# Cross-entropy of 256 x 32000 logits: the first 64 rows in three loads instead of two

## The chip, the cores and the metric

The kernel runs on one core of one Trainium2 chip. The metric is the time of one execution on the device in microseconds. The kernel before takes 82.59 us, the median of four runs (82.54 to 82.75).

A core has several engines that run side by side, each with its own instruction queue: TensorE (PE in the profile), VectorE (DVE), ScalarE (ACT), GpSimd (POOL) and SyncE (SP). Here SP only issues transfers. Sixteen DMA engines move data between the chip's main memory (HBM) and the core's own memory (SBUF), which has 128 partitions.

## What is computed

For each of 256 rows, the logarithm of the sum of the exponentials of the row, less the logit of the row's label:

```python
def reference(logits, labels):           # [256, 32000] float32, [256] int32
    log_probs = logits - np.max(logits, axis=-1, keepdims=True)
    log_probs = log_probs - np.log(np.sum(np.exp(log_probs), axis=-1, keepdims=True))
    return np.array([-log_probs[i, labels[i]] for i in range(batch)])
```

The kernel leaves out the maximum: it computes log(sum(exp(x)) * exp(-x[label])), which is the same number. The input is 32.77 MB, each element is read once, and the output is 1 KB.

## The kernel before

**Groups and chunks.** The rows are cut into four groups of 64, 128, 32 and 32 rows (`GROUPS`, L18). A group of k rows lies over all 128 partitions: each row is cut into 128/k stretches, one to a partition. The first group so has 16000 columns on each partition, the second 32000, the last two 8000 each. `LOADS` (L20 to L25) cuts the columns of each group into chunks, and each chunk is one load from HBM: 14 in all, numbered through. A load of n columns is 128 rows of 4n bytes.

**Buffers.** Chunks 0 to 5 have a buffer each (`SLOTS`, L30). Chunks 6 and 7 use the buffers of chunks 2 and 3 again. The six chunks of the last group (`TAIL`, from chunk 8) lie side by side in the buffer of chunk 1 (`TAIL_SLOT`, L32).

**Work on a chunk** (`step`, L270). ScalarE takes the exponential in place (`exps`, L208 to L215). For the first group the same instruction also sums over the columns into one column of `parts`. For chunks 2 to 11 (`HALVED`, L41) VectorE adds the two halves of the chunk and sums the result into `near` (L294). Chunks 12 and 13 are summed by ScalarE again. For every chunk after the first group, TensorE multiplies the sums of the partitions by `weights` (L300), which gives one number for each row. For the first group that is done once, after its last chunk: a sum over `parts` (L284) and one product (L285). Its logarithm (L222) is taken after the exponential of the next chunk.

**The label's logit.** ACT's queue loads the labels (L229). POOL computes the addresses and gathers the logits of the labels from HBM (L250). In the step of chunk `GATHERED` (1) ScalarE takes exp(-x) of these (L274), and VectorE and TensorE build `weights` from them (L276 to L282). That is why the row's sum comes out multiplied by exp(-x[label]).

**Warm-up.** In the step of chunk `WARM_FROM` (7) TensorE gets sixteen products whose result nobody uses (L291).

**Order.** All is in an order written out by hand. SP first issues the loads of chunks 0 to 5. Then comes a loop (L307) that, for each later load, first writes out the steps up to the one that frees its buffer. So load 6 waits for VectorE's half-sum of chunk 2, load 7 for that of chunk 3, and the tail loads stand behind load 7 on SP's queue; their buffer is free as soon as ScalarE has worked on chunk 1. Each load also has a completion counter. There are eight of these, handed round among the loads, the transfer of the labels and the store of the result. A load that takes a used counter waits for the transfer that had it before.

**Start and end.** `begin_first_load_before_barrier` puts the first load ahead of the barrier at the start. `end_before_store_lands` (L60) puts SP's waits for everything else ahead of the store of the result, so that the barrier and the clearing of the counters run while the store is under way. The last instruction is SP's wait for the store. Because the clearing must leave out the store's counter, and this is the last one of the range here, the range is shortened by one (L91, L92).

Of the kernel before, what the change touches and what calls it, by code (L numbers as in the profile page):

```python
# [17 lines left out]
GROUPS = [64, 128, 32, 32]  # L18

LOADS = [  # L20
    [1024, 14976],
    [8896, 8192, 8320, 6592],
    [4736, 3264],
    [2496, 1824, 1344, 992, 736, 608],
# [2 lines left out]
GROUP_OF = [g for g, ns in enumerate(LOADS) for _ in ns]  # L27


SLOTS = [0, 1, 2, 3, 4, 5, 2, 3]  # L30
TAIL = len(SLOTS)
TAIL_SLOT = 1  # L32
SKIP = 32


WARM_FROM = 7
WARM = 16

GATHERED = 1

HALVED = range(2, 12)  # L41


def begin_first_load_before_barrier(nc):
# [15 lines left out]
def end_before_store_lands(nc):  # L60

    body, end = nc.m.functions[0].blocks[1:3]
    insts = list(body.instructions)
    at = max(k for k, i in enumerate(insts) if i.opcode == "DMACopy")
    store = insts[at]
    (landed,) = store.sync_info.on_update
    assert store.engine == mybir.EngineType.SP  # L70
    assert all(i.engine != mybir.EngineType.SP or i.opcode != "DMACopy" for i in insts[at + 1:])

    rest = list(end.instructions)
    drain = rest.pop(0)
    assert drain.engine == mybir.EngineType.SP and drain.opcode == "Drain"
    waits = list(drain.sync_info.on_wait)
    (full,) = [w for w in waits if w.id == landed.id]

    held = {w.id: w.wait_value for w in store.sync_info.on_wait}
    waits = [w for w in waits if w.id != landed.id and held.get(w.id) != w.wait_value]  # L80
    assert not list(drain.sync_info.on_update)
    insts.insert(at, mybir.InstEventSemaphore(
        name=drain.name, engine=drain.engine, debug=drain.debug, ins=[], outs=[],
        sync_info=mybir.SyncInfo(on_wait=waits, on_update=[]),
    ))

    clear = next(k for k, i in enumerate(rest) if i.opcode == "ISA")
    old = rest[clear]
    assert old.op_name == "EVENT_SEMAPHORE_RANGE_CLEAR"
    words, fields = list(old.instr), dict(old.ant_dict)  # L90
    assert words[14] == fields["range_last"] == landed.id  # L91
    words[14] = fields["range_last"] = landed.id - 1  # L92
    rest[clear] = mybir.InstISA(
        isa_opcode=old.isa_opcode, instr=tuple(words), verify=old.verify, op_name=old.op_name,
        ant_dict=fields, ant_isa_is_sequencer_only=old.ant_isa_is_sequencer_only,
        name=old.name, engine=old.engine, debug=old.debug, ins=[], outs=[],
    )

    assert all(i.opcode in ("Drain", "EventSemaphore") for i in rest[clear + 1:])
    del rest[clear + 1:]  # L100
    rest.append(mybir.InstEventSemaphore(
        name=nc.get_next_instruction_name(), engine=mybir.EngineType.SP, debug=old.debug,
        ins=[], outs=[],
        sync_info=mybir.SyncInfo(
            on_wait=[full],
            on_update=[mybir.SyncUpdate(
                sync_type="semaphore", id=full.id, ant_name=full.ant_name,
                update_mode="sem-sub-imm", update_value=full.wait_value,
            )],
        ),  # L110
    ))
    body.instructions = insts
    end.instructions = rest
# [3 lines left out]
def kernel(  # L117
# [6 lines left out]
    nc = tc.nc  # L124
    nc.at_finalize(begin_first_load_before_barrier)
    nc.at_finalize(end_before_store_lands)
    B, C = logits.shape
    assert B == P * ROWS == sum(GROUPS)
# [19 lines left out]
    width = {}  # L148
    for i, s in enumerate(SLOTS):
        width[s] = max(width.get(s, 0), CHUNKS[i])  # L150
    width[TAIL_SLOT] = max(width[TAIL_SLOT], sum(CHUNKS[TAIL:]))


    place = []
    for i, s in enumerate(SLOTS):
        skip = SKIP if s == 0 else 0
        t = big.tile([P, skip + width[s]], F32, name=f"x{i}", tag=f"slot{s}")
        place.append(t[:, skip:skip + CHUNKS[i]])
    assert all(width[s] % 64 == 0 for s in width)
    tail = big.tile([P, width[TAIL_SLOT]], F32, name="x_tail", tag=f"slot{TAIL_SLOT}")  # L160
    for i in range(TAIL, last + 1):
# [3 lines left out]

    assert HALVED[0] == last_of[0] + 1 and HALVED[-1] == last - 2
    assert all(CHUNKS[i] % 2 == 0 for i in HALVED)
    parts = small.tile([P, len(LOADS[0])], F32, name="parts")
    row_0 = small.tile([P, 1], F32, name="row_0")
    near = {i: small.tile([P, 1], F32, name=f"near{i}") for i in range(HALVED[0], last + 1)}  # L170
    res = small.tile([1, B], F32, name="res")
# [36 lines left out]
    def exps(i):  # L208
        if i in HALVED:
            acc = None  # L210
        elif i > last_of[0]:
            acc = near[i][:, :]
        else:
            acc = parts[:, i:i + 1]
        nc.scalar.activation(out=place[i], in_=place[i], func=AF.Exp, accum_out=acc)  # L215
# [5 lines left out]
    def logs(rows, sums):  # L221
        nc.scalar.activation(out=res[0:1, rows], in_=sums, func=AF.Ln)  # L222

    with tc.manual_schedule():
        first = len(set(SLOTS))
        for i in range(first):
# [43 lines left out]
        def step(i):  # L270
            exps(i)
            g = GROUP_OF[i]
            if i == GATHERED:
                nc.scalar.activation(out=eg[:, :], in_=g_at[:, :], func=AF.Exp, scale=-1.0)  # L274
                for r in range(ROWS):
                    nc.vector.tensor_scalar_mul(diag[r][:, :], ident[:, :], eg[:, r:r + 1])  # L276

                for r in range(ROWS):
                    nc.tensor.matmul(  # L279
                        spread[:, r * P:(r + 1) * P], ones[:, :], diag[r][:, :], start=True, stop=True  # L280
                    )
                nc.vector.tensor_mul(out=weights[:, :], in0=holds[:, :], in1=spread)  # L282
            if i == last_of[0]:
                nc.vector.reduce_sum(out=row_0[:, :], in_=parts[:, :], axis=mybir.AxisListType.X)  # L284
                nc.tensor.matmul(lane[0], row_0[:, :], weigh(0), start=True, stop=True)  # L285
            if i == last_of[0] + 1:
                logs(slice(0, row_at[1]), lane[0])
            if i == WARM_FROM:
                col = place[i][:, CHUNKS[i] - 1:CHUNKS[i]]
                for _ in range(WARM):  # L290
                    nc.tensor.matmul(warm, col, diag[0][:, :], start=True, stop=True)  # L291
            if i in HALVED:
                half = CHUNKS[i] // 2
                nc.vector.scalar_tensor_tensor(  # L294
                    out=place[i][:, 0:half], in0=place[i][:, 0:half], scalar=1.0,
                    in1=place[i][:, half:CHUNKS[i]],
                    op0=mybir.AluOpType.mult, op1=mybir.AluOpType.add, accum_out=near[i][:, :],
                )
            if g:
                nc.tensor.matmul(  # L300
                    lane[g], near[i][:, :], weigh(g), start=i == first_of[g], stop=i == last_of[g]
                )


        assert GATHERED <= last_of[0]
        done = 0
        for i in range(first, last + 1):  # L307
            slot = SLOTS[i] if i < TAIL else TAIL_SLOT
            while done <= SLOTS[:first].index(slot):
                step(done)  # L310
# [40 lines left out]
```

## Time and profile before

| What | Value |
|---|---|
| Profiled execution | 82.58 us |
| Its span, first to last instruction | 80.9 us |
| ScalarE busy | 57.4 us (71%) |
| VectorE busy | 27.6 us (34%) |
| TensorE busy | 12.0 us (15%) |
| Mean HBM rate over the span | 405 GB/s |
| ScalarE waiting for loads, in four waits | 21.4 us |

The span's 40 slices in the page are about 2 us each; a digit is the busy share in tenths. The landing time of a load is its issue time plus the "us to landing" of the DMA view. In the tables by stage, the columns are the length, then busy time of PE, PEld (the weight loads of TensorE), DVE, ACT and POOL, each with its number of instructions, then the granted clock, the DMA share and the rate in GB/s.

Two rows of ScalarE set the scale: 1024 columns take 1.06 us and 14976 take 12.68 us. A load of the same columns takes longer than that: the 8320 columns land 9.86 us after the load before them, and ScalarE works on them for 7.14 us.

### The profile page before, as it was taken

How to read it: one execution, taken by the hardware profiler on the slowest of the kernel's cores; microseconds unless marked ns; L12 is line 12 of the kernel's file. 1: busy time of each engine (PE TensorE's matmuls, PEld its weight loads, DVE VectorE, ACT ScalarE, POOL GpSimd, SP SyncE). 2: the span in 40 equal slices, each digit the busy share in tenths (PEclk: the TensorE clock that was granted, in tenths of full speed). 3: DMA queues.
4: the chain of work that ended last, by engine and by line, in shares of the span. 5: the costliest groups of instructions: out<-in, count | busy, mean ns of one | idle time of the engine just before them, and what ended most of it. 6: DMA issues, size and time to landing. Idle time of an engine off the chain costs nothing.

```text
span 80.9 us, 261 instructions
## 1 busy us (share of the span) xinstructions
PE 12.0 (15%) x66; PEld 6.6 (8%) x66; DVE 27.6 (34%) x28; ACT 57.4 (71%) x23; POOL 5.2 (6%) x20
## 2 busy tenths in 40 slices
PE   0040000000000000061000020020000201159981
PEld 0030000000000000040000000000000000035550
DVE  1100000000000000030039908930099198898870
ACT  6230000000399999999999991599979999999993
POOL 4038810000000000000000000000000000000000
PEclk9999999999999999999999999999999999999998
DMA  4999997599979696997996997999999999999940
GB/s 87 647 474 474 474 444 326 237 415 474 528 317 563 281 563 292 486 518 324 453 526 296 493 510 306 417 456 469 421 412 412 427 432 402 439 414 408 417 164 1
DMA packets 2084, 32.77 MB, mean 405 GB/s; under 512 B 290, under 2 KB 291, under 8 KB 1060
## 3 DMA queue, kind: packets, MB, share of 16 engines
q1 hardware_dynamic: 2018, 32.77, 95.1%
q0 software_dynamic: 64, 0.00, 0.1%
q10 hardware_dynamic: 2, 0.00, 0.0%
HBM read 32.77 MB, written 0.00 MB: 405 GB/s over the span
## 4 chain that ended last, share of the span: by engine, by line
DMA 61%; ACT 34%; SPq 1%; another core or an unknown queue 1%; issue 1%; PE 0%
DMA x<-in_logits_dram 61%; ACT x L215 24%; ACT x_tail L215 9%; SPq L206 1%; PE bank L300 0%; ACT res L222 0%
## 5 line engine op out<-in xcount | busy, mean ns | idle before, releaser
L215 ACT ACTIVATE x<-x 128x1024 f32<-128x1024 f32 (+7 forms) x8 | 48.1, 6030 | 21.4 <-DMA x<-in_logits_dram 21.4
L294 DVE SCALAR_TENSOR_TENSOR x<-x 128x4448 f32<-128x4448 f32 (+5 forms) x6 | 21.8, 3631 | 15.3 <-ACT x L215 15.3
L276 DVE TENSOR_SCALAR diag<-ident,eg 128x128 f32<-128x128 f32 x2 | 0.5, 286 | 29.4 <-ACT eg L274 29.4
L300 PE MATMUL bank<-weights,near 128*1 128x32 f32 (+1 forms) x24 | 3.5, 262 | 33.1 <-DVE x L294 32.4
L215 ACT ACTIVATE x_tail<-x_tail 128x2496 f32<-128x2496 f32 (+5 forms) x6 | 7.4, 1301 | 0.0
L291 PE MATMUL bank<-diag,x 128*1 128x128 f32 x32 | 6.2, 383 | 0.0
L279 PE MATMUL bank<-diag,ones 128*128 128x128 f32 x4 | 1.2, 461 | 29.9 <-DVE diag L276 29.9
L294 DVE SCALAR_TENSOR_TENSOR x_tail<-x_tail 128x1248 f32<-128x1248 f32 (+3 forms) x4 | 4.1, 1024 | 0.6 <-ACT x_tail L215 0.3
L300 PEld LDWEIGHTS bank<-weights,near 128*1 128x1 f32 x24 | 1.0, 82 | 35.7 <-DVE x L294 34.6
L291 PEld LDWEIGHTS bank<-diag,x 128*1 128x1 f32 x32 | 3.6, 115 | 2.4
L279 PEld LDWEIGHTS bank<-diag,ones 128*128 128x128 f32 x4 | 0.9, 322 | 30.0 <-DVE diag L276 30.0
L250 POOL DMA_INDIRECT g_at<-in_logits_dram,idx x2 | 2.1, 1030 | 0.6 <-issue 0.3
L198 ACT ACT_TABLE_LOAD x1 | 1.3, 1283 | 0.8 <-PEq L335 0.8
L239 PE MATMUL bank<-one,lbl_row 1*128 1x1 f32 x4 | 1.0, 352 | 3.9 <-DVE lbl_row L237 3.9
L239 PEld LDWEIGHTS bank<-one,lbl_row 1*128 1x128 f32 x4 | 0.9, 317 | 3.9 <-DVE lbl_row L237 3.9
L237 DVE CAST lbl_row<-words 1x256 f32<-1x256 int32 x1 | 0.3, 281 | 2.4 <-DMA words<-in_labels_dram 2.4
L265 POOL TENSOR_SCALAR_AFFINE_SELECT holds<-holds 128x32 f32<-128x32 f32 (+2 forms) x4 | 1.0, 238 | 0.3
L261 POOL TENSOR_SCALAR_AFFINE_SELECT holds<-holds 128x32 f32<-128x32 f32 (+2 forms) x4 | 1.0, 239 | 0.1
L282 DVE TENSOR_TENSOR weights<-holds,bank 128x256 f32<-128x256 f32 x1 | 0.4, 422 | 1.2 <-PE bank L279 1.2
L222 ACT ACTIVATE res<-bank 1x64 f32<-1x64 f32 (+2 forms) x3 | 0.7, 219 | 0.1
L242 DVE CAST lbl<-bank 128x2 int32<-128x2 f32 x1 | 0.2, 160 | 1.1 <-PE bank L239 1.1
L294 DVE DVE_READ_ACCUMULATOR x<-x 128x1 f32 x6 | 0.5, 83 | 0.0
(18 smaller groups left out, 3.7 us busy)
## 6 DMA issues: line engine op xcount, KB each, us to landing
x<-in_logits_dram SPq DMA_DIRECT2D x1, 7488.0 KB, 20.6
x<-in_logits_dram SPq DMA_DIRECT2D x1, 4448.0 KB, 30.7
x<-in_logits_dram SPq DMA_DIRECT2D x1, 4160.0 KB, 49.3
x<-in_logits_dram SPq DMA_DIRECT2D x1, 4096.0 KB, 39.9
x<-in_logits_dram SPq DMA_DIRECT2D x1, 3296.0 KB, 56.5
x<-in_logits_dram SPq DMA_DIRECT2D x1, 2368.0 KB
x<-in_logits_dram SPq DMA_DIRECT2D x1, 1632.0 KB, 15.3
x_tail<-in_logits_dram SPq DMA_DIRECT2D x1, 1248.0 KB
```

The source lines that it names most:

```text
L198: nc.scalar.preload_act_table_set("natural_log_exp_and_others")
L206: nc.sync.dma_start(out=place[i], in_=flat[GROUP_OF[i]][:, a:a + CHUNKS[i]])
L215: nc.scalar.activation(out=place[i], in_=place[i], func=AF.Exp, accum_out=acc)
L222: nc.scalar.activation(out=res[0:1, rows], in_=sums, func=AF.Ln)
L239: nc.tensor.matmul(lbl_up[:, r:r + 1], lbl_row[:, r * P:(r + 1) * P], one[:, :], start=True, stop=True)
L250: nc.gpsimd.indirect_dma_start(out=g_at[:, r:r + 1], out_offset=None, in_=logits[:, :], in_offset=bass.IndirectOffsetOnAxis(ap=idx[:, r:r ...
L261: nc.gpsimd.affine_select(out=h, in_=h, pattern=[[-q, k]], base=0, channel_multiplier=1, compare_op=mybir.AluOpType.is_ge, fill=0.0,)
L265: nc.gpsimd.affine_select(out=h, in_=h, pattern=[[q, k]], base=q - 1, channel_multiplier=-1, compare_op=mybir.AluOpType.is_ge, fill=0.0,)
L279: nc.tensor.matmul(spread[:, r * P:(r + 1) * P], ones[:, :], diag[r][:, :], start=True, stop=True)
L291: nc.tensor.matmul(warm, col, diag[0][:, :], start=True, stop=True)
L294: nc.vector.scalar_tensor_tensor(out=place[i][:, 0:half], in0=place[i][:, 0:half], scalar=1.0, in1=place[i][:, half:CHUNKS[i]], op0=mybir. ...
L300: nc.tensor.matmul(lane[g], near[i][:, :], weigh(g), start=i == first_of[g], stop=i == last_of[g])
```

## The change

The first group's second chunk, 14976 columns, becomes two chunks of 4992 and 9984. All later chunks keep their sizes and move up by one number, so the constants that name chunks move too. There are now 15 loads, of which SP issues seven at once. The tail uses the buffer of the 9984 columns. `GATHERED` follows the last chunk of the first group, so exp(-x) of the gathered logits stands after the exponential of the 9984 columns. `parts` has three columns.

With one transfer more, the store of the result gets another of the eight counters, one in the middle of the range that is cleared at the end. So the clearing is written as two instructions, one below and one above that counter.

```diff
 LOADS = [
-    [1024, 14976],
+    [1024, 4992, 9984],
     [8896, 8192, 8320, 6592],
     [4736, 3264],
     [2496, 1824, 1344, 992, 736, 608],
...
-SLOTS = [0, 1, 2, 3, 4, 5, 2, 3]
+SLOTS = [0, 1, 2, 3, 4, 5, 6, 3, 4]
 TAIL = len(SLOTS)
-TAIL_SLOT = 1
+TAIL_SLOT = 2
...
-WARM_FROM = 7
+WARM_FROM = 8
...
-GATHERED = 1
-
-HALVED = range(2, 12)
+GATHERED = 2
+
+HALVED = range(3, 13)
...
-    assert words[14] == fields["range_last"] == landed.id
-    words[14] = fields["range_last"] = landed.id - 1
-    rest[clear] = mybir.InstISA(
...
+    bounds = old.ant_dict["range_first"], old.ant_dict["range_last"]
+    assert bounds[0] < landed.id < bounds[1]
+
+    def clearing(ends):
+        words, fields = list(old.instr), dict(old.ant_dict)
+        assert (words[13], words[14]) == bounds
+        words[13], words[14] = fields["range_first"], fields["range_last"] = ends
+        return mybir.InstISA(
...
-    del rest[clear + 1:]
+    rest[clear:] = [clearing((bounds[0], landed.id - 1)), clearing((landed.id + 1, bounds[1]))]
```

More of the change, by code (lines that the diff above doesn't have):

```diff
@@ L89, in end_before_store_lands @@
     assert old.op_name == "EVENT_SEMAPHORE_RANGE_CLEAR"
-    words, fields = list(old.instr), dict(old.ant_dict)
-    assert words[14] == fields["range_last"] == landed.id
-    words[14] = fields["range_last"] = landed.id - 1
-    rest[clear] = mybir.InstISA(
[L94 to L97, printed above, removed]
+    bounds = old.ant_dict["range_first"], old.ant_dict["range_last"]
[5 more added lines that the diff above has]
+        return mybir.InstISA(
+            isa_opcode=old.isa_opcode, instr=tuple(words), verify=old.verify, op_name=old.op_name,
+            ant_dict=fields, ant_isa_is_sequencer_only=old.ant_isa_is_sequencer_only,
+            name=nc.get_next_instruction_name(), engine=old.engine, debug=old.debug, ins=[], outs=[],
+        )
     assert all(i.opcode in ("Drain", "EventSemaphore") for i in rest[clear + 1:])
-    del rest[clear + 1:]
+    rest[clear:] = [clearing((bounds[0], landed.id - 1)), clearing((landed.id + 1, bounds[1]))]
     rest.append(mybir.InstEventSemaphore(
```

## The prediction

> **What bounds the kernel now.** I read the page first (engine shares and the 40 slices), then the chain that ended last in order of time, then ScalarE's timeline, then the DMA issues with their landings, and last the end of the program.
>
> ```profile
> span 80.9 us, 261 instructions
> ...
> ACT  6230000000399999999999991599979999999993
> ...
> DMA  4999997599979696997996997999999999999940
> ...
> q1 hardware_dynamic: 2018, 32.77, 95.1%
> ```
>
> The load queue q1 fills 95.1% of 16 engines' span, while ScalarE is idle for the first quarter and has a hole later. So the question is which of the two sets the end. The chain answers:
>
> ```profile
> 2.12 49.27 DMA x<-in_logits_dram
> ...
> 51.42 7.14 ACT x L215
> 58.56 0.62 another core or an unknown queue
> ...
> 59.20 5.61 ACT x L215
> ...
> 64.85 3.87 ACT x L215
> ...
> 68.91 2.91 ACT x L215
> 71.82 7.46 ACT x_tail L215 x8
> ```
>
> Up to 51.42 us the chain is one stretch of DMA. After that it names ScalarE, but each start up to 59.20 is a landing: at 51.42 (the 8320 columns) and at 59.18 (the 6592). The ScalarE timeline shows how its early work sits in that stream:
>
> ```profile
> 21.47 12.68 ACT L215 ACTIVATE x<-x 128x14976 f32<-128x14976 f32 x1 [16.62 <-DMA x<-in_logits_dram]
> ...
> 34.24 7.60 ACT L215 ACTIVATE x<-x 128x8896 f32<-128x8896 f32 x1
> ...
> 41.85 7.01 ACT L215 ACTIVATE x<-x 128x8192 f32<-128x8192 f32 x1
> 51.42 7.14 ACT L215 ACTIVATE x<-x 128x8320 f32<-128x8320 f32 x1 [2.55 <-DMA x<-in_logits_dram]
> 59.20 5.70 ACT L215 ACTIVATE x<-x 128x6592 f32<-128x6592 f32 x1 [0.65 <-DMA x<-in_logits_dram]
> ```
>
> The reader is to see the brackets. ScalarE is late once: the 8896 columns are begun at 34.24, though they landed at 1.18 (issue) + 30.7 (to landing) = 31.88, so it is 2.4 us behind. At the 8192 columns, landed at 1.66 + 39.9 = 41.56 and begun at 41.85, it is 0.3 behind. Then it stands still for 2.55 us at 51.42 and 0.65 us at 59.20. Whatever the big first piece costs has been paid back by 51.42.
>
> The end follows the stream too. Issue starts come from SP's timeline (53.36, 54.21, 55.16, 59.20), times to landing from the DMA issues:
>
> ```profile
> x<-in_logits_dram SPq DMA_DIRECT2D x1, 1632.0 KB, 15.3
> ...
> x_tail<-in_logits_dram SPq DMA_DIRECT2D x1, 912.0 KB, 19.6
> ...
> x_tail<-in_logits_dram SPq DMA_DIRECT2D x1, 496.0 KB, 21.6
> ...
> x_tail<-in_logits_dram SPq DMA_DIRECT2D x1, 304.0 KB, 19.2
> ```
>
> That is 68.66, 73.81, 76.76 and 78.4 us, and ScalarE begins those chunks at 68.91, 73.90, 76.76 and 78.48. From 59.20 on, ScalarE works without a gap and every chunk lands 0 to 0.25 us before its turn: stream and ScalarE are both tight there. So the end moves with the landing times after 59 us and with nothing before.
>
> **What the Trainium skill says.** "DMA: Bandwidth & Descriptors", section "Where 436 GB/s comes from", gives 435.2 GB/s as the ceiling of the fabric. The stages of the trace agree: 432 GB/s from 9.60 to 21.47 us, 433 from 31.90 to 41.60. The section "Anatomy of one DMA" puts about 2 us of fixed cost on a DMA, but nearly all of it in the confirmation of the last byte, not in setting up. The trace agrees that this doesn't add up along a queue: the loads of 8192, 8320 and 6592 columns land 9.68, 9.86 and 7.73 us apart, 1.18 ns a column each, with no 2 us between. "ScalarE: Activation LUTs", section "What ACT_TABLE_LOAD costs", prices an ACTIVATE at 186 ns plus 0.833 ns a column, with back-to-back ones overlapping by about 93 ns. The trace's 14976 columns in 12.68 us and 1024 in 1.06 us give 0.833 ns a column, the same.
>
> **The change part by part.** First the split of 14976 into 4992 and 9984. Bytes are unchanged. ScalarE's pieces, by the slope above from the 1024 row: 1.057 + 3968 x 0.8332 ns = 4.36 us, and 1.057 + 8960 x 0.8332 ns = 8.52 us, together 12.88 against 12.68. With its reading of the accumulator (186 ns) that is about 0.3 us more work after overlap, and all of it lies in idle time. In time: 4992 columns land at 3.7 + 4992 x 1.182 ns = 9.6, done 14.0. The 9984 land where the 14976 landed, about 21.5, done 30.0, with the gathered exponent (L274) after it at 30.2 instead of 34.15. ScalarE then waits for the 8896 until 31.9, ends them at 39.5 (41.8 before), waits for the 8192 until 41.6, ends them at 48.6 (48.87 before), and is again waiting at 51.4. So the 2.4 us of lateness become idle time and the next thing that is late is the same landing as before.
>
> VectorE ends the half-sum of the 8896 columns at 39.6 + 4.8 = 44.4 (46.67 before), which lets SP issue the 4736 columns then and not at 46.70. The stream does not wait for this issue: at 46.7 the rest of the 8320 and the 6592 are still queued, 12.5 us until 59.2. An earlier issue only lengthens the queue. The load of 3264 is issued near 53.1 (53.36 before), with 6 us of the 6592 still queued. The five tail loads follow on SP, and the sixth (608) waits for the counter of the load eight before it. In the trace SP stops 3.1 us there, until the 6592 columns have landed at 59.18. With one load more in front, eight back is again the 6592. Same place, same landing; it has 19.2 us to land, so it isn't starved.
>
> One more issue on SP at the start costs 0.4 to 0.5 us by the rows there; SP has issued the last of seven near 3.6 us, and the one that is later by this is wanted only after 21 us. On the queue behind it stands nothing until 44 us. The gather on POOL (first and last issue 5.6 and 7.1, 9.1 to 12.2 us to landing, so by about 19) is wanted at 30.0 now: 11 us of cover. The 128 x 3 sum of parts and the shifted indices cost nothing: they sit beside ScalarE's wait.
>
> What is not hidden is the cost of one load more in a stream that is never empty: 128 row packets and their closing writes. From the landings: 31.88 to 59.15 holds 23104 columns in three loads, 68.66 to 78.4 holds 8000 columns in six. Two equations, 23104r + 3c = 27.27 and 8000r + 6c = 9.74, give r = 1.1725 ns a column and c = 0.06 us a load. The four smallest alone (3680 columns in 4.59 us) give 0.07. Bounds: zero, if a load between long ones costs nothing, because the small ones may lose for another reason; 0.15, twice what the smallest ones show. I take 0.06, and all later landings shift by it.
>
> The second part is the end: one range clear becomes two, on POOL.
>
> ```profile
> L346 SPq EVENT_SEMAPHORE  x7: 17/28/28, 75.5 to 80.9; - x7
> ...
> L346 POOLq EVENT_SEMAPHORE_RANGE_CLEAR  x1: 138/138/138, 80.6 to 80.6; - x1
> ```
>
> The clear runs from 80.6 to 80.74, and SP's last wait, for the result's store, is over at 80.9. A second 138 ns ends at 80.88, so it lies just under the store's landing. Bounds 0 to 0.14 (the whole clear, if POOL's end counts later than it shows); I take 0.01. The page's 80.9 has a rounding of 0.05, so the cover is thin.
>
> Sum: the profiled execution took 82.58 us (80.9 of span, 1.68 around it); 82.58 + 0.06 + 0.01 = 82.65. The median of before is 82.59, practically the same execution, so 82.65 stands as the forecast, +0.07%. A measurement of this kernel tells about 0.2% from no change, 0.165 us here: this is inside it.
>
> **Rivals.** (1) ScalarE's earlier start does count. If its 2.4 us of lateness at 34.24 reached the end, the time would be 82.65 - 2.4 = 80.25. Against it stands the 2.55 us wait at 51.42, which absorbs the lateness whole; I give it 0.03.
>
> (2) The stream runs better in the middle. These stages show a dip:
>
> ```profile
> 31.90:41.60 9.70, 1.60 (x6) 1.01 (x6) 0.97 (x4) 9.70 (x4) 0.00 (x0) 1.00 1.00 433
> 41.60:51.42 9.82, 0.58 (x2) 0.09 (x2) 7.32 (x3) 7.27 (x4) 0.00 (x0) 1.00 0.98 423
> ```
>
> If 423 against 433 GB/s (the last two columns are DMA share and GB/s) came from the reissue at 46.70, or from queues running thin, an earlier issue would win 9.82 x (1 - 423/433) = 0.23 us: 82.65 - 0.23 = 82.42. Against it: the landings of that stage, 9.86 us for 8320 columns, show 1.185 ns a column, only 0.07 us over the 1.177 of the other stages. 0.11.
>
> (3) The other side: the second clear on POOL becomes the end. Its price is 0.138 us, with the 0.06 of the load 82.58 + 0.14 + 0.06 = 82.78; it decides as soon as the store lands before POOL has finished, that is when the gap of 80.74 to 80.9 is not real or the program's end follows POOL. For it: the margin is 0.02 us. Against it: SP's wait is shown as later. 0.24, which holds also the case that a middle load costs its upper bound of 0.15 us (82.74).
>
> (4) The change doesn't do what it says for the work order: should the last tail load wait for the 4736 columns instead of the 6592, it would be issued near 64.9 (ScalarE begins them at 64.85). Its turn on the queue is at 77.6, so 13 us of queued bytes still cover it, and the time stays 82.65; it needs no chance of its own.
>
> **How the numbers follow.** Forecast 0.62 (82.55 to 82.75); gains of both kinds 0.14; losses 0.24. The range takes 82.42 of the second rival at its lower edge and 82.82 above, the third rival with 0.04 for the spread among runs. Faster 0.14, same 0.62, slower 0.24.
>
> **What would show it.** ScalarE begins a 4992 chunk near 9.6 us and one of 9984 near 21.5. It waits near 30 and near 39.7, and at 51.4 and 59.2 as before, later by 0.03 to 0.1 us. q1 has 2018 + 144 = 2162 packets (128 rows and 16 closing ones per load, as 14 x 144 = 2016 is now). POOL shows two range clears, the last ending at or before SP's last event. The prediction is wrong if the 6592 columns land more than 0.15 us away from 59.15, if ScalarE shows gaps after 59.2, or if the span's end is POOL's.

## The result and the profile after

The changed kernel takes 82.68 us, the median of 33 runs, beside 82.59 us for the kernel before (54 runs). The ratio over the runs is 1.002, with a 95% interval of 1.0011 to 1.003 (that of the medians is 1.0011). So it is slower by 0.09 to 0.25 us. That lies at the 0.2% at which a change of this kernel can just be told from none. The profiled execution of the changed kernel took 82.79 us, above its own median; this matters below.

The head of the page of the changed kernel:

```profile
span 81.1 us, 266 instructions
...
ACT  6140299000399991999649990599979999999993
...
q1 hardware_dynamic: 2162, 32.77, 94.9%
```

The reader is to see that ScalarE now has work in the fifth to seventh slice and pays for it with new holes further on. The load queue carries 144 packets more, as forecast, and is as full as before. ScalarE's timeline shows the holes one by one (start, length, and in brackets the idle time before):

```profile
9.68 4.36 ACT L220 ACTIVATE x<-x 128x4992 f32<-128x4992 f32 x1 [4.74 <-DMA x<-in_logits_dram]
...
21.61 8.52 ACT L220 ACTIVATE x<-x 128x9984 f32<-128x9984 f32 x1 [7.47 <-DMA x<-in_logits_dram]
...
32.10 7.62 ACT L220 ACTIVATE x<-x 128x8896 f32<-128x8896 f32 x1 [1.78 <-DMA x<-in_logits_dram]
...
41.75 7.03 ACT L220 ACTIVATE x<-x 128x8192 f32<-128x8192 f32 x1 [1.93 <-DMA x<-in_logits_dram]
51.57 7.14 ACT L220 ACTIVATE x<-x 128x8320 f32<-128x8320 f32 x1 [2.79 <-DMA x<-in_logits_dram]
59.34 12.68 ACT L220 ACTIVATE x<-x 128x6592 f32<-128x6592 f32 x3 [0.64 <-DMA x<-in_logits_dram]
```

ScalarE is no longer late at the 8896 columns: it starts at 32.10 instead of 34.24. It then waits for the 8192, and from the 8320 columns on it is where it was, 0.15 us later (51.57 instead of 51.42). The chain that ended last has the same members as before, with one issue of SP more in front:

```profile
2.64 48.91 DMA x<-in_logits_dram
...
51.57 7.14 ACT x L220
...
59.34 5.67 ACT x L220
...
72.03 7.42 ACT x_tail L220 x8
```

The two clears of the counters, in the view of the instructions of the program's end (count, then shortest, median and longest in ns, then first and last start in us):

```profile
L351 SPq EVENT_SEMAPHORE  x7: 17/28/28, 75.7 to 81.1; - x7
...
L351 POOLq EVENT_SEMAPHORE_RANGE_CLEAR  x2: 49/90/131, 80.8 to 80.9; - x2
```

The same view, first from 80.8 to 80.86 us and then from 80.87 to 81.05, shows them one by one:

```profile
L351 POOLq EVENT_SEMAPHORE_RANGE_CLEAR  x1: 49/49/49, 80.8 to 80.8; - x1
...
L351 POOLq EVENT_SEMAPHORE_RANGE_CLEAR  x1: 131/131/131, 80.9 to 80.9; - x1
```

The first, below the store's counter, takes 49 ns, and the second, above it, 131 ns. Both start before SP's last wait, which ends at 81.1 us. By this view the second clear is covered.

### The profile page after: what moved, and what is told of

Its sections match the earlier page's. It is cut to its first block, busy times and chain, and to the rows that moved or that the text cites. A ratio compares the mean times of both kernels' runs of the same rounds, so it can differ in the third digit from the quotient of the medians.

```text
span 81.1 us, 266 instructions
## 1 busy us (share of the span) xinstructions
PE 11.7 (14%) x66; PEld 6.5 (8%) x66; DVE 27.6 (34%) x28; ACT 57.9 (71%) x25; POOL 5.2 (6%) x20
## 3 DMA queue, kind: packets, MB, share of 16 engines
q1 hardware_dynamic: 2162, 32.77, 94.9%
## 4 chain that ended last, share of the span: by engine, by line
DMA 60%; ACT 33%; SPq 2%; issue 1%; another core or an unknown queue 1%; PE 0%
DMA x<-in_logits_dram 60%; ACT x L220 24%; ACT x_tail L220 9%; SPq L211 2%; PE bank L305 0%; ACT res L227 0%
## 5 line engine op out<-in xcount | busy, mean ns | idle before, releaser
L220 ACT ACTIVATE x<-x 128x1024 f32<-128x1024 f32 (+8 forms) x9 | 48.4, 5387 | 21.1 <-DMA x<-in_logits_dram 21.1
L220 ACT ACTIVATION_READ_ACCUMULATOR x<-x 128x1 f32 x3 | 0.6, 186 | 0.0
```

## The experiments

Two causes were in question: the one load more in the stream (theory A in the expectations), and the one clear more at the end (theory B). Each run has its own kernel before on the same chip; the medians of these were 82.63, 82.63 and 82.60 us in the three sets.

**The clear alone.** The kernel before, with its one clear divided in two. The line is set against the changed kernel's; `middle` is the third counter of the range, and the store's counter is again the last:

```diff
-    rest[clear:] = [clearing((bounds[0], landed.id - 1)), clearing((landed.id + 1, bounds[1]))]
+    rest[clear:] = [clearing((bounds[0], middle)), clearing((middle + 1, landed.id - 1))]
```

> The kernel before with only the end of the change: the counters are cleared in two instructions instead of one. Theory A (a cost per load in the stream): no change, ratio 1.000, the wait for the store still ends last. Theory B (the second clear costs): slower by 0.05 to 0.14 us, ratio 1.0006 to 1.0017, and POOL's last clear ends after SP's last wait has begun to stand alone.

It took 82.68 us beside 82.63: ratio 1.0011, 0.9992 to 1.003. That tells nothing apart. But its profile shows something else. This kernel has the transfers of the kernel before without any difference, and yet:

```profile
21.70 12.68 ACT L221 ACTIVATE x<-x 128x14976 f32<-128x14976 f32 x1 [17.00 <-DMA x<-in_logits_dram]
```

The first group landed at 21.70 us here and at 21.47 in the profile of before. This execution took 82.91 us, 0.23 us above the median of its own kernel. So landing times of two single profiles can't be compared to a tenth of a microsecond, and the 0.14 us between 21.47 and 21.61 in the two traces above is no measure of the load. What can be compared is the rest of each execution, which turned out to be steady. For each profiled execution the table has the start of the last piece of the first group, the issue of the store, and the time of the whole execution. The last column is the time of the execution less the issue of the store, so it holds the 1.7 us that lie outside the span:

| Profiled kernel | Clears | First group begun | Store issued | Execution | Between the first two | After the store's issue |
|---|---|---|---|---|---|---|
| before | 1 | 21.47 | 79.79 | 82.58 | 58.32 | 2.79 |
| changed | 2 | 21.61 | 79.95 | 82.79 | 58.34 | 2.84 |
| changed, again | 2 | 21.58 | 79.98 | 82.83 | 58.40 | 2.85 |
| clear alone | 2 | 21.70 | 80.05 | 82.91 | 58.35 | 2.86 |
| transfer alone | 2 | 21.93 | 80.21 | 83.06 | 58.28 | 2.85 |
| nine transfers | 1 | 21.90 | 80.19 | 82.97 | 58.29 | 2.78 |
| one load | 2 | 22.00 | 80.34 | 83.19 | 58.34 | 2.85 |
| nine clears | 9 | 21.41 | 79.73 | 83.00 | 58.32 | 3.27 |
| labels by POOL | 1 | 21.57 | 79.88 | 82.64 | 58.31 | 2.76 |

From the first group to the store, all of them need 58.28 to 58.40 us, whatever ScalarE did before. From the store to the end, kernels with one clear need 2.76 to 2.79 and those with two 2.84 to 2.86. The four profiles with another first load, further below, all have one clear and give 58.33 to 58.37 and 2.77 to 2.78. That made the clear a suspect, to be tried with a larger dose.

**The transfer alone.** The 14976 columns come in two transfers, while ScalarE works on them in one piece; with the end of the change, because the store has the same counter as there:

```diff
+PIECES = {1: [4992, 9984]}
...
-        nc.sync.dma_start(out=place[i], in_=flat[GROUP_OF[i]][:, a:a + CHUNKS[i]])
+        for n in PIECES.get(i, [CHUNKS[i]]):
+            nc.sync.dma_start(
+                out=place[i][:, at:at + n], in_=flat[GROUP_OF[i]][:, a + at:a + at + n]
+            )
+            at += n
```

> The chunk of 14976 stays one piece of work for ScalarE, but comes in two transfers, 4992 and 9984, with the end of the change. Theory A: as the changed kernel, +0.06 us or a little more (ratio about 1.001 to 1.002), all landings from 21.5 us on later by it. Theory C (ScalarE's earlier and divided work in the first 30 us disturbs the stream): no change against before, because ScalarE still begins at 21.5 us.

82.80 us, ratio 1.0013, 0.9989 to 1.0037. Its ratio is near that of the changed kernel, but the interval holds no change as well. So it doesn't tell the theories apart, and a disturbance of the stream by ScalarE's early work (theory C) is not excluded by it. The changed kernel has that early work, and its stretch from the first group to the store, 58.34 and 58.40 us, is that of the others to within 0.12 us; a disturbance before 21.6 us would not show in it.

**Nine transfers.** The same with nine transfers of 1664 columns, which gives the store the last counter again and so leaves the end of the kernel before, with one clear:

```diff
+PIECES = {1: [1664] * 9}
```

> The chunk of 14976 comes in nine transfers of 1664; the store then has the last counter again, so the end is that of before with one clear. Theory A: eight loads more at 0.06 us each, +0.48 us, ratio 1.006, the landing of the chunk later by this. Theory B: no change at all. If what counts is not the load but a single displacement of the first landing (0.09 us in the changed kernel's trace), about +0.1 us.

82.96 us, ratio 1.0034, 1.0014 to 1.0054. The stream has eight loads more; after the store nothing changed (2.78 us in the table). The load queue of this kernel, and the landing of the nine:

```profile
q1 hardware_dynamic: 3170, 32.77, 95.4%
```

```profile
21.90 12.68 ACT L221 ACTIVATE x<-x 128x14976 f32<-128x14976 f32 x1 [17.01 <-DMA x<-in_logits_dram]
```

1152 packets more are 8 times 144. The queue's share did not fall: 95.4% of 81.4 us are 77.7 us in packets on each engine, against 76.9 (95.1% of 80.9) before. So the loss is not a gap in the queue: the same bytes took longer. By the medians it is 0.33 us for eight, 0.04 us a load; by the interval of the ratio 0.015 to 0.056. So loads do cost, but less than the 0.06 us of the prediction, which the interval excludes. The 0.04 is an average over eight loads of 1664 columns; whether it goes with the loads or with their 144 packets each was not tried apart. That the one load of the change costs as much is worked out and not shown: its queue has 94.9% of 81.1 us, 77.0 us in packets, which is no more than before within the rounding.

**Nine clears.** The kernel before with nine clears instead of one, eight of two counters and the last of what is left. The lines are again set against the changed kernel's:

```diff
-    rest[clear:] = [clearing((bounds[0], landed.id - 1)), clearing((landed.id + 1, bounds[1]))]
+    cuts = list(range(bounds[0], bounds[0] + 17, 2)) + [landed.id]
+    rest[clear:] = [clearing((p, q - 1)) for p, q in zip(cuts, cuts[1:])]
```

> The kernel before with its clear of the counters divided into nine instructions. So far, the time between the issue of the store and the end of the execution is 2.79 and 2.78 us in the two profiled kernels with one clear, and 2.84, 2.85, 2.85 and 2.86 us in the four with two. Theory B (the end of the program follows POOL, the second clear costs about 0.065 us): eight clears more cost about 0.5 us, ratio 1.006. Theory A (clears are hidden under the store's landing): the first two or three are free and the rest shows, 0.2 to 0.35 us, ratio 1.003 to 1.004.

83.09 us, ratio 1.0061, 1.0039 to 1.0082: 0.46 us for eight clears more. The end of the program:

```profile
L352 POOLq EVENT_SEMAPHORE_RANGE_CLEAR  x9: 45/45/51, 80.6 to 81.2; - x9
...
L352 SPq EVENT_SEMAPHORE  x7: 17/28/28, 75.5 to 80.9; - x7
```

Here the last clear starts at 81.2, after SP's last wait at 80.9. If only the visible excess counted, about 0.3 us would show, just below the interval of the ratio (0.32 to 0.68 us). The table has 3.27 - 2.79 = 0.48 us, 0.06 for each clear, and with two clears 0.05 to 0.1 us more than with one.

The start and length of each clear in nanoseconds, from the trace's records, tell which of the two engines the end follows. From the end of POOL's last clear to the end of the execution there are 1.76 to 1.80 us in all thirteen profiled executions, whether with one, two or nine clears (the time of the execution less the time of that end in the span, so what lies ahead of the first instruction is in it). From SP's last wait there are 1.60 to 1.64 us with one clear, 1.68 to 1.70 with two and 2.10 with nine. So the end of the execution follows POOL, and SP's later wait for the store covers nothing of the clears. From the start of the first clear to the end of the last, POOL needs 0.14 us with one, 0.19 to 0.21 with two and 0.63 with nine: 0.06 us for each clear more. Why the end follows POOL is not seen in the trace; it lies in the 1.7 us outside the span.

**The change with one clear.** The labels are loaded from POOL's queue instead of ACT's. The eight counters are handed round among the transfers of SP and ACT, so the store now gets the last one, and the end of the kernel before fits:

```diff
-        nc.scalar.dma_start(
+        nc.gpsimd.dma_start(
             out=words[:, :], in_=bass.AP(tensor=lbl_words, offset=0, ap=[[2 * B, 1], [1, 2 * B]])
         )
```

> The changed kernel with the labels loaded from POOL's queue instead of ACT's. The store then has the last counter again, so one clear is enough; the labels come later, with about 10 us of cover. Theory B: 0.065 us faster than the changed kernel, ratio to before 1.0003 to 1.001. Theory A: the same as the changed kernel, ratio to before 1.001 to 1.002.

> The changed kernel again on this chip, for the comparison. By the sum of one load (0.04 us, an eighth of what nine transfers cost) and one clear (0.065 us) the ratio is 1.0013; the landing of the 9984 columns plus 61.18 us gives the time of its profiled execution.

With the labels by POOL 82.66 us, ratio 0.9999, 0.9985 to 1.0013; the changed kernel beside it 82.70 us, 1.0011, 0.9997 to 1.0025. The difference has the expected sign; the intervals overlap, and 0.9999 lies below what either theory gave. The 1.0011 is near the 1.0013 of the sum. The rule for the profiled execution of the changed kernel gave 21.58 + 61.18 = 82.76 us, and it took 82.83, so it holds to 0.07 us. The profile of the first has one clear again, and 2.76 us after the store:

```profile
L346 POOLq EVENT_SEMAPHORE_RANGE_CLEAR  x1: 138/138/138, 80.7 to 80.7; - x1
```

**Fewer loads.** If each load costs 0.04 us, one load for the whole first group should gain. The constants that name chunks move down by one, the tail's buffer begins 32 columns further in, and the store gets a middle counter, so there are two clears:

```diff
-    [1024, 14976],
+    [16000],
...
-SLOTS = [0, 1, 2, 3, 4, 5, 2, 3]
+SLOTS = [0, 1, 2, 3, 4, 1, 2]
```

> The first group comes in one load of 16000 columns, 13 loads in all, with two clears at the end. Theory A: 0.06 us faster than before, 0.15 faster than the changed kernel (ratio to before about 0.999); ScalarE is late by 2.9 us at the 8896 columns and has caught up at the 8320. Theory B: slower than before by the clear, 1.001. If ScalarE's lateness reached the end it would be slower by 0.7 us or more.

This expectation failed under every theory: 83.20 us, ratio 1.0069, 1.0051 to 1.0088, slower by 0.57 us. Its ScalarE timeline:

```profile
22.00 13.54 ACT L220 ACTIVATE x<-x 128x16000 f32<-128x16000 f32 x1 [19.92 <-DMA x<-in_logits_dram]
...
51.98 7.14 ACT L220 ACTIVATE x<-x 128x8320 f32<-128x8320 f32 x1 [1.73 <-DMA x<-in_logits_dram]
59.77 12.59 ACT L220 ACTIVATE x<-x 128x6592 f32<-128x6592 f32 x3 [0.66 <-DMA x<-in_logits_dram]
```

ScalarE has caught up by 51.98, where it waits 1.73 us. Its lateness, although the largest of all kernels, isn't the cause. The first group itself lands half a microsecond late, at 22.00 us. So the size of the first load was suspected of a price of its own. Three sizes were tried in the kernel before, each with 14 loads and one clear; only the first row of `LOADS` changes, to `[2048, 13952]`, `[4096, 11904]` and `[8192, 7808]`.

> The kernel before with its first group cut into 2048 and 13952 columns: the same number of loads and one clear. If only the number of loads counts, no change (ratio 1.000). If the size of the first load matters, as the 0.57 us lost with one load of 16000 suggests, the first group lands later, by up to 0.3 us, or earlier, by as much as the slow start of the 1024 is worth (0.1 us).

> The kernel before with its first group cut into 2048 and 13952, again, to see whether 0.9992 (0.998 to 1.0003) is a gain. If the first piece of 2048 helps, 0.9990 to 0.9998 again; if not, 1.000.

> The first group cut into 4096 and 11904. If the 0.5 us that the one load of 16000 loses grows with the size of the first load, +0.1 us (ratio 1.001). If the loss comes only with very long rows, no loss; if the slow start of the 1024 is what 2048 mends, 0.999.

> The first group cut into 8192 and 7808. If the loss grows with the size of the first load, +0.24 us (ratio 1.003); if it comes only with very long rows, 0.999 to 1.000. The group lands near 21.4 us in both, later by the loss.

| First load, columns | Median, us | Ratio to before (interval) |
|---|---|---|
| 1024 | 82.59 to 82.63 | 1 |
| 2048 | 82.60 | 0.9992 (0.998 to 1.0003) |
| 2048, again | 82.60 | 0.9996 (0.9986 to 1.0005) |
| 4096 | 82.59 | 1.0003 (0.9995 to 1.0011) |
| 8192 | 82.84 | 1.0029 (1.0017 to 1.0041) |
| 16000, two clears | 83.20 | 1.0069 (1.0051 to 1.0088) |

No loss is shown up to 4096 columns; then it is 0.24 us at 8192 and 0.57 at 16000, of which 0.06 is the second clear. A loss proportional to the size would be 0.1 us at 4096, where the interval ends at 0.09, so that is only just excluded.

The load queues of the last two kernels, first 8192 and then 16000 columns, have 94.8% of 81.2 us and 94.6% of 81.5 us:

```profile
q1 hardware_dynamic: 2018, 32.77, 94.8%
...
q1 hardware_dynamic: 1874, 32.77, 94.6%
```

That is 77.0 and 77.1 us in packets, against 76.9 before, while the spans grew by 0.3 and 0.6. So, other than with nine transfers, most of what was added is time in which the engines had no packet. Why a long first load brings that about isn't settled by these runs. None of the kernels tried is shown to beat the kernel before.

## Why the prediction was right

**The bound.** The prediction rested on one reading: ScalarE's lateness of 2.4 us is absorbed by its wait for the 8320 columns, so the end follows the landings. The changed kernel shows it: ScalarE begins the 8896 columns 2.1 us earlier, and the end doesn't come earlier. The second column from the right of the table says the same over nine executions: ScalarE was done with the first group early (30.1 us, the changed kernel), late (34.2, before) and very late (35.5, one load), and the stretch to the store stayed within 0.12 us. The first rival, a gain of 2.4 us, had the landing against it and fell.

**The times in ScalarE's order.** Forecast were 9.6, 21.5, a wait near 30 and one near 39.7; the trace has 9.68, 21.61, a wait of 1.78 us before 32.10 and one of 1.93 before 41.75. The load of 4736 columns was issued at 44.58 (44.4 forecast). The last load of the tail went out at 59.34, on the landing of the 6592 columns, by the count of eight. SP's timeline has both:

```profile
44.58 0.33 SPq L211 DMA_DIRECT2D x<-in_logits_dram  x1
...
59.34 0.33 SPq L211 DMA_DIRECT2D x_tail<-in_logits_dram  x1
```

The packets, 2162, are exact.

**The dip in the middle** (second rival). The rate from 41.60 to 51.42 us was 423 GB/s in the changed kernel's trace too, so the earlier issue of the 4736 columns gave nothing:

```profile
41.60:51.42 9.82, 0.58 (x2) 0.09 (x2) 5.56 (x3) 7.03 (x1) 0.00 (x0) 1.00 0.98 423
```

**The load.** Taken at 0.06 us from two equations on the landings; eight more loads cost 0.33 us, 0.04 each. The estimate leaned on the short loads at the tail and was half as large again as that; the 0.04 lies inside the bounds that were given. The changed kernel without its second clear, labels by POOL, shows 0.03 us, with an interval from a gain of 0.12 to a loss of 0.11, so the price of a single load is not shown alone.

**The clear.** Taken at 0.01 us, because the view put SP's last wait after it; it measured 0.06. This is the step that was wrong: "it lies just under the store's landing". The clear was indeed over before SP's wait, as the list of signs asked, and cost its time all the same, because the end follows POOL. The third rival named this and bounded the price by the length of the whole clear, 0.138 us. The change makes no second clear of that length: its two take 49 and 131 ns, with 27 ns between them, so POOL is done 0.07 us later than with one of 138. How long a clear takes goes with the counters that it covers: with the clear alone, three counters took 51 ns and the rest of the range 117.

The sum of both terms is 0.04 + 0.06 = 0.10 us. The medians differ by 0.09, and the interval of the ratio is 0.09 to 0.25, so there may be more that these runs do not show. The forecast 0.07 was of the right size and its parts were not: one too large, one too small. That their errors nearly cancelled is luck; that the end would stand still for ScalarE's earlier work is not.

One part of the list of signs was a trap: the prediction said that a landing of the 6592 columns more than 0.15 us away from 59.15 would prove it wrong. The chain has that landing 0.17 us late, at 59.32, but a kernel with unchanged transfers had its first group late by 0.23 in one profile, so a single landing can't prove it either way.

The prediction also took 2 us of fixed cost for a transfer from the Trainium skill, "DMA: Bandwidth & Descriptors", section "Anatomy of one DMA". That section is on transfers that GpSimd issues in software; these loads are issued by SP on the queue marked `hardware_dynamic`. So what carries the reading is the spacing of the landings in the trace alone.

## What to carry to other kernels

Before giving an engine its work earlier, look for its next long wait on a transfer: what it gains before that wait is lost in it, and here 2.1 us of earlier work bought nothing. A change of order is then worth only its side costs, so price those: every load in a full stream, and every instruction added at the program's end, even where another engine's wait seems to cover it, as it seemed to cover the clears here. For effects of a tenth of a microsecond, multiply the suspect by eight, and compare stretches within each execution instead of the landings of two.

## What the runs showed that was not expected

- A clear of counters on POOL adds 0.06 us to the execution although SP's last wait is shown as later (0.46 us for eight). The execution ends 1.76 to 1.80 us after POOL's last clear in all thirteen profiles, while its distance from SP's last wait goes from 1.60 to 2.10 us. Clears of two or three counters take 45 to 51 ns, the one of the whole range 138.
- The time of landing of the first group varies between executions with the same transfers by up to 0.29 us (21.41, 21.47 and 21.70 us), and with it the time of the execution. From there to the store's issue the stretch is 58.28 to 58.40 us in all of the table.
- A first load of 8192 or 16000 columns costs 0.24 and about 0.5 us against one of 1024 to 4096, although fewer or as many loads are made. The time that the DMA engines spend in packets hardly grows with it (77.0 and 77.1 us against 76.9); the time is added between packets.
